# Two-layer diffusion block on one core: the modulation's weight product made by scaled copies and additions instead of matmuls

## The chip, the core and the metric

The kernel runs on one core of a Trainium2 chip. The core has a matrix engine (TensorE, PE in the profile, with its weight loads as PEld), VectorE (DVE), ScalarE (ACT), GpSimd (POOL) and SyncE (SP, which here only issues DMAs). Each engine works through its own queue in order and waits on semaphores for the others. TensorE reads from SBUF and writes to PSUM; GpSimd reads and writes SBUF only. The metric is the time of one execution on the device in microseconds, lower is better.

## What is computed

Two layers of a block: a modulated RMSNorm, one wide input projection that feeds a state-space scan and a differential attention, two gated branch projections, an output projection, and a modulated gated FFN with a short convolution. There are 256 latent tokens and 256 context tokens; both go through the same weights in layer 0, and in layer 1 the context is only read. All data is fp32. The change concerns the modulation, which is a product of a vector with a large matrix:

```python
for i in range(DEPTH):
    mod_l = (jax.nn.silu(c) @ w_mod[i] + b_mod[i])[:, None, :]
    mod_c = (jax.nn.silu(c_ctx) @ w_mod[i] + b_mod[i])[None, None, :]
    sh1_l, sc1_l, g1_l, sh2_l, sc2_l, g2_l = jnp.split(mod_l, N_MOD, axis=-1)
    ...
```

`w_mod[i]` has 1024 rows and 6144 columns (25 MB a layer). `c` and `c_ctx` are the two conditions. The second, small part of the change is in the scan: for each chunk of 128 tokens it needs the running sum of `a` in both directions and the sums over the rest of the chunk (`a_cs` and `a_cs[..., -1:] - a_cs` in the reference's `ssd_scan`).

## The kernel before

**Projections.** A projection takes its weights in tiles of 4 blocks of 128 rows by 256 columns (512 KB). `load_w` issues a tile's DMA on SP's queue (buffers `raw`, 3), `split_w` makes a rounded copy `whi` on ACT (L313) and the rest `wlo` on DVE (L314), 3 buffers each, and the gemm helpers (L384 to L445) run three matmuls per block of rows: high by high, high by low, low by high. `plan` lists all tiles in order. `take` hands tiles to a gemm, keeps `DL` = 2 tiles loaded or ready ahead, and calls `drip` once for each tile. A tile of 512 tokens is 24 matmuls of 512 columns.

**What runs between.** `lanes` are two queues of generators (attention heads, scan groups) that a gemm advances by `pump` after every second block of rows; so heads and scan run in between the projections' matmuls. `trickle` is a third queue, advanced by `drip`: it holds the modulation.

**The modulation.** The first third of a layer's columns (`g` = 0) of layer 0 is made at the start (`boot_mod`). The other five groups of 2048 columns, two of layer 0 and the first of layer 1 during layer 0 and two during layer 1, are made by `mod_part` (L457). `s2` holds for each block of 128 rows the two conditions after their activation as two columns among 32, the others zero. One step loads a block of 128 rows by 1024 columns (`mraw`, 512 KB, 2 buffers) and does 4 fp32 matmuls (L465), each with 32 columns of `s2` as weights and 256 columns of the block moving, into 4 bands of 32 partitions of the PSUM bank `pmmod`; 16 steps sum one group. An fp32 matmul is two records in the trace, so a step is 8. Then the bank is copied to `modrow`, transposed in four pieces (L472) and added to the bias. Five groups are 80 steps.

**Order.** The instructions of each engine are ordered by a scheduling framework that follows the program's order where it can; attention and scan matmuls (`pmm`, `ptr`, L85 and L88) are kept in program order. No queue is reordered at run time.

**Stages.** Layer 0: start (0 to 66 us of the span), attention with the Q, K and V projections (to 235), the "dt block", a short chain that makes the step sizes and the triangle sums `p1` (L817 to L863, near 235 to 250), the B, C and gate projections and the attention's branch projection (to 425), the scan with the XS, gate and Z projections (to 590), the last gates and the scan's branch projection (to 665), then output projection and FFN. Layer 1 begins near 1097 and goes the same way, with 256 tokens in most projections. `flush` empties `trickle` at the end of the scan's branch projection.

Of the kernel before, what the change touches and what calls it, by code (L numbers as in the profile page):

```python
# [10 lines left out]
F32 = mybir.dt.float32  # L11
# [21 lines left out]
C_ID, C_ONE, C_LE, C_GE, C_GT, C_LT, C_COS, C_SIN = 0, 128, 256, 384, 512, 640, 768, 1024  # L33
C_W = 1280


def shape_constants():
    a = np.zeros((P, C_W), np.float32)
    i = np.arange(P)
    r, s = i[:, None], i[None, :]  # L40
    a[:, C_ID:C_ID + P] = r == s
    a[:, C_LE:C_LE + P] = r <= s
    a[:, C_GE:C_GE + P] = r >= s
    a[:, C_GT:C_GT + P] = r > s
    a[:, C_LT:C_LT + P] = r < s
# [14 lines left out]
def hybrid_backbone_kernel(  # L60
# [36 lines left out]
    strict = (kt[:, C_GT:C_GT + P], kt[:, C_LT:C_LT + P])  # L97
# [3 lines left out]
    V.memset(mhalf, -0.5)  # L101

# [226 lines left out]
    trickle = []  # L329

# [29 lines left out]
    def take(n_tiles):  # L360
# [5 lines left out]
        for _ in range(n_tiles):  # L366
            drip()
# [89 lines left out]
    def mod_part(i, g, pool, ps):  # L457

        for half in range(2):
            for k in range(KD):  # L460
                raw = pool.tile([P, 4, 256], F32, tag="mraw", name=nm("mraw"), bufs=2)
                src = w_mod[i, k * P:(k + 1) * P, g * 2048:(g + 1) * 2048]
                nc.sync.dma_start(raw, src.rearrange("p (j h n) -> p h j n", j=4, h=2)[:, half])
                for j in range(4):
                    T.matmul(ps[32 * j:32 * j + 32, half * 256:half * 256 + 256], s2[:, k, :], raw[:, j, :],  # L465
                             start=k == 0, stop=k == KD - 1)
                yield 1
        row = lp.tile([P, 512], F32, tag="g", name=nm("modrow"), bufs=4)
        A.copy(row, ps)
        pt = bank("s")  # L470
        for b in range(4):
            T.transpose(pt[:, b * P:(b + 1) * P], row[:, b * P:(b + 1) * P], ident)  # L472
        m = col[i]["mod"]
        for v in range(2):
            V.tensor_tensor(
                m[:, g * 16:(g + 1) * 16, v].rearrange("p (j b) -> p b j", j=4),
                pt.rearrange("p (b j r) -> p b j r", b=4, j=4)[:, :, :, v],
                col[i]["bm"][:, g * 16:(g + 1) * 16].rearrange("p (j b) -> p b j", j=4), op=ALU.add)
        if g == 0:
            a, sc, nw = col[i]["a1"], m[:, 8:16, :], col[i]["n1"]  # L480
        elif g == 2:
            a, sc, nw = col[i]["a2"], m[:, 32:40, :], col[i]["n2"]
        else:
            return
        V.scalar_tensor_tensor(a, sc, 1.0, nw.unsqueeze(2).to_broadcast([P, KD, 2]), op0=ALU.add, op1=ALU.mult)
# [89 lines left out]
    for i in range(DEPTH):  # L575
# [75 lines left out]
        trickle.extend(mod_part(*lg, mp, mb) for lg in (((0, 1), (0, 2), (1, 0)) if full else ((1, 1), (1, 2))))  # L651
# [17 lines left out]
        spare[:] = ["mm"]  # L669
        ast = ExitStack()  # L670
# [141 lines left out]


# [5 lines left out]
        if True:  # L819
# [24 lines left out]
            for n, lhs in enumerate((tri[0], tri[1], strict[0], strict[1])):  # L844
                T.matmul(p1[:, n * P:(n + 1) * P], lhs, av, start=True, stop=True)
            T.matmul(p2[:, 0:P], ones, av, start=True, stop=True)
            p1v = p1.rearrange("p (n t c) -> p n t c", n=4, t=4)
# [42 lines left out]

        spare[:] = ["mm"]
# [154 lines left out]
        spare[:] = ["mm", "s"]  # L1046
        rst = ExitStack()
# [159 lines left out]
```

## Time and profile before

| | us |
|---|---|
| median of 3 runs | 1742.55 |
| lowest, highest | 1740.89, 1753.69 |
| profiled execution, its own time | 1740.01 |
| its span, first to last instruction | 1738.2 |
| TensorE clock granted in it, mean | 0.993 |

The busy time of an engine is the union of its instructions' times, without waits. A group's row has the line, the engine, the operation, output and inputs, the shapes and a count; then busy time and mean of one in ns; then the idle time of the engine just before these instructions, and who ended it. In a row of windows each engine has its busy time in that stretch and a count of instructions. A tile's row has the shortest, median and longest duration in ns. The end of a matmul is modelled, so what it holds PE for is read from one start to the next.

### The profile page before, as it was taken

The numbers are of one execution on the slowest core, as the hardware profiler recorded it, in microseconds if no ns is written. First come the engines' busy times: TensorE is split into PE (matmuls) and PEld (weight loads), VectorE is DVE, ScalarE is ACT, GpSimd is POOL, SyncE is SP. The second block draws the span as 40 slices with busy tenths as digits, with TensorE's granted clock in tenths as the row PEclk, the third lists the DMA queues.
The fourth block names the chain that finished last, engine by engine and source line by source line (L and its number), as shares of the span: only waits on it lengthen the run. The fifth ranks groups of instructions, "written<-read, shape, count | busy, mean of one in ns | idle before, by whom it ended". The sixth has DMA issues, their size and how long they took to land. (4 is left out here: it accounts for less than half of the span.)

```text
span 1738.2 us, 27022 instructions
## 1 busy us (share of the span) xinstructions
PE 1667.1 (96%) x10547; PEld 1406.2 (81%) x10547; DVE 1148.0 (66%) x2008; ACT 848.2 (49%) x1567; POOL 181.3 (10%) x212
## 2 busy tenths in 40 slices
PE   7999999999988999999999999999999898989997
PEld 4788878777766788888888888788879788989997
DVE  4776667325988855766666326666675789779964
ACT  3565665413545423644444225555655455466653
POOL 3000010001433000300000002100000252010000
PEclk9999999999999999999999999999999999989999
DMA  9644333555443234233323335844535445646653
GB/s 317 215 127 126 115 119 108 166 173 146 121 107 100 74 109 146 74 97 97 97 87 95 92 108 161 255 146 146 152 93 171 121 110 144 199 154 185 193 176 117
DMA packets 233199, 240.71 MB, mean 138 GB/s; under 512 B 10908, under 2 KB 223551, under 8 KB 233071
## 3 DMA queue, kind: packets, MB, share of 16 engines
q1 hardware_dynamic: 230720, 237.14, 45.4%
q8 instruction: 83, 1.36, 0.3%
q0 software_dynamic: 1312, 1.03, 0.2%
q10 hardware_dynamic: 1039, 0.81, 0.1%
q14 instruction: 45, 0.37, 0.1%
HBM read 234.62 MB, written 4.33 MB: 137 GB/s over the span
## 5 line engine op out<-in xcount | busy, mean ns | idle before, releaser
L314 DVE TENSOR_TENSOR wlo<-raw,whi 128x1024 fp32r<-128x1024 f32 (+1 forms) x318 | 388.3, 1221 | 255.7 <-ACT whi L313 254.8
L313 ACT CAST whi<-raw 128x1024 fp32r<-128x1024 f32 (+1 forms) x318 | 329.2, 1036 | 378.4 <-PE pmmmm L408 146.6
L407 PE MATMUL pmmmm<-th,whi 128*128 128x512 f32 x744 | 306.3, 412 | 1.6 <-DVE chv L572 1.6
L408 PE MATMUL pmmmm<-tl,whi 128*128 128x512 f32 x744 | 296.5, 399 | 0.0
L409 PE MATMUL pmmmm<-th,wlo 128*128 128x512 f32 x744 | 295.6, 397 | 0.0
L407 PEld LDWEIGHTS pmmmm<-th,whi 128*128 128x128 f32 x744 | 140.5, 189 | 42.2 <-issue 7.9
L409 PEld LDWEIGHTS pmmmm<-th,wlo 128*128 128x128 f32 x744 | 140.4, 189 | 34.5 <-issue 1.0
L408 PEld LDWEIGHTS pmmmm<-tl,whi 128*128 128x128 f32 x744 | 140.5, 189 | 31.0 <-issue 2.2
L393 PE MATMUL pmmmm<-th,whi 128*128 128x256 f32 x480 | 138.5, 289 | 1.5 <-ACT whi L313 1.3
L395 PE MATMUL pmmmm<-th,wlo 128*128 128x256 f32 x480 | 134.7, 281 | 0.6 <-DVE wlo L314 0.6
L394 PE MATMUL pmmmm<-tl,whi 128*128 128x256 f32 x480 | 134.8, 281 | 0.0
L969 POOL TENSOR_TENSOR cs<-cs,csc 128x512 f32<-128x512 f32 x48 | 69.1, 1454 | 264.0 <-DMA cs<-csd 141.5
L393 PEld LDWEIGHTS pmmmm<-th,whi 128*128 128x128 f32 x480 | 90.7, 189 | 6.2 <-issue 3.8
L394 PEld LDWEIGHTS pmmmm<-tl,whi 128*128 128x128 f32 x480 | 90.8, 189 | 0.7 <-issue 0.4
L395 PEld LDWEIGHTS pmmmm<-th,wlo 128*128 128x128 f32 x480 | 90.6, 189 | 0.8 <-DVE wlo L314 0.8
L409 PE MATMUL psmm<-th,wlo 128*128 128x512 f32 x200 | 79.3, 397 | 0.0
L725 ACT ACTIVATE e<-psscore,nmx 128x512 f32<-128x512 f32 (+1 forms) x96 | 58.1, 610 | 43.5 <-DVE nmx L722 40.5
L408 PE MATMUL psmm<-tl,whi 128*128 128x512 f32 x200 | 79.2, 396 | 0.0
L521 POOL TENSOR_TENSOR rs<-ms,mhalf 128x2 f32<-128x2 f32 x9 | 6.3, 699 | 698.5 <-DVE ms L518 698.5
L407 PE MATMUL psmm<-th,whi 128*128 128x512 f32 x200 | 79.0, 395 | 0.0
L722 DVE TENSOR_REDUCE nmx<-psscore 128x1 f32<-128x512 f32 (+1 forms) x80 | 51.8, 684 | 34.3 <-PE psscore L85 34.2
L441 PE MATMUL pmmmm<-whi,th 128*128 128x256 f32 x256 | 74.3, 290 | 0.0
(346 smaller groups left out, 3899.0 us busy)
## 6 DMA issues: line engine op xcount, KB each, us to landing
raw<-in_w_in_dram SPq DMA_DIRECT2D x124, 512.0 KB, 4.0
raw<-in_w_up_dram SPq DMA_DIRECT2D x88, 512.0 KB, 3.6
mraw<-in_w_mod_dram SPq DMA_DIRECT2D x80, 512.0 KB, 4.7
raw<-in_w_down_dram SPq DMA_DIRECT2D x45, 512.0 KB, 3.6
cs<-csd SPq DMA_DIRECT2D x24, 512.0 KB, 5.8
boot<-in_w_mod_dram SPq DMA_DIRECT2D x16, 512.0 KB, 9.3
raw<-in_w_br_att_dram SPq DMA_DIRECT2D x16, 512.0 KB, 3.6
raw<-in_w_br_ssd_dram SPq DMA_DIRECT2D x16, 512.0 KB, 3.5
```

What stands on the lines that cost most here:

```text
L313: pin(A.copy(hi[:, 0:n, :], raw[:, 0:n, :]))
L314: pin(V.tensor_tensor(lo[:, 0:n, :], raw[:, 0:n, :], hi[:, 0:n, :].bitcast(F32), op=ALU.subtract))
L393: T.matmul(o[f], whi[:, kk, cs], xh, start=first, stop=False)
L394: T.matmul(o[f], whi[:, kk, cs], xl, start=False, stop=False)
L395: T.matmul(o[f], wlo[:, kk, cs], xh, start=False, stop=last)
L407: T.matmul(o, whi[:, k % 4, cs], hi[k][:, 0:n], start=k == 0, stop=False)
L408: T.matmul(o, whi[:, k % 4, cs], lo[k][:, 0:n], start=False, stop=False)
L409: T.matmul(o, wlo[:, k % 4, cs], hi[k][:, 0:n], start=False, stop=k == k_tiles - 1)
L441: T.matmul(b[:, n, :], hi[k][:, ts], whi[:, k % 4, :], start=k == 0 and n == 0, stop=False)
L722: V.tensor_reduce(nmx[:, cc, 0:ng], sc[cc].rearrange("p (g k) -> p g k", g=ng), axis=AX.X, op=ALU.max, negate=True)
L725: A.activation(e[cc][:, g * w:(g + 1) * w], sc[cc][:, g * w:(g + 1) * w], AF.Exp, bias=nmx[:, cc, g:g + 1], accum_out=sm[:, cc, g:g + 1])
L969: G.tensor_tensor(cs[:, dr], cs[:, dr], csc[:, t, 16 * dr + 4 * g:16 * dr + 4 * g + 4].unsqueeze(2).to_broadcast([P, 4, P]), op=ALU.subtract)
```

## The change

`mod_part` no longer multiplies on TensorE. It takes the 2048 columns of a group in 4 blocks of 512. For each of the 8 blocks of 128 rows it loads 128 rows by 512 columns (`mraw`, 256 KB, 2 buffers), and ACT multiplies this tile by a condition: each partition's row by that partition's value of `s2`, a copy with a column as scale. The first row block's products go straight into the sum `macc`; from then on GpSimd adds each product to `macc`. With two conditions (`nv` = 2) the first product goes to a scratch tile `mt` (1 buffer) and the second back into `mraw`; with one it goes into `mraw`. So a step is one DMA, `nv` products and `nv` additions (none at the first row block). After 8 steps 4 matmuls with `pick` as weights (one column of ones among zeros, shifted so that the four blocks fall on different partitions) sum `macc` over its partitions. `macc` has one buffer. A group is 32 steps instead of 16, each with half the bytes. In layer 1 only the latent condition is made (`nv` = 1).

`pace` sets how many steps are advanced: `drip` is called `pace`/2 times per weight tile. It is 4 in the attention of layer 0, 3 until the scan, 0 in the scan, 4 from the end of the scan until layer 1 sets 3.

In the dt block two of four triangle products go: the strict sums are the other triangle's sums less the value itself, two subtractions on DVE and one exponential where there were two.

```diff
@@ shape_constants and its use: the two strict triangles go, the constant is 1024 wide instead of 1280
+    pick = base.tile([P, 64], F32, name="pick")
+    V.memset(pick, 0.0)
+    V.memset(pick[:, 32:33], 1.0)
...
         for _ in range(n_tiles):
-            drip()
+            owed[0] += pace[0]
+            while owed[0] >= 2:
+                owed[0] -= 2
+                drip()
...
-    def mod_part(i, g, pool, ps):
+    def mod_part(i, g, pool, ps, nv):
-        for half in range(2):
+        for q in range(4):
+            acc = pool.tile([P, nv, 512], F32, tag="macc", name=nm("macc"), bufs=1)
             for k in range(KD):
-                raw = pool.tile([P, 4, 256], F32, tag="mraw", name=nm("mraw"), bufs=2)
-                src = w_mod[i, k * P:(k + 1) * P, g * 2048:(g + 1) * 2048]
-                nc.sync.dma_start(raw, src.rearrange("p (j h n) -> p h j n", j=4, h=2)[:, half])
-                for j in range(4):
-                    T.matmul(ps[32 * j:32 * j + 32, half * 256:half * 256 + 256], s2[:, k, :], raw[:, j, :],
-                             start=k == 0, stop=k == KD - 1)
-                yield 1
+                raw = pool.tile([P, 512], F32, tag="mraw", name=nm("mraw"), bufs=2)
+                c0 = g * 2048 + q * 512
+                nc.sync.dma_start(raw, w_mod[i, k * P:(k + 1) * P, c0:c0 + 512])
+                yield 1
+                for v in range(nv):
+                    sum_ = acc[:, v, :]
+                    if k == 0:
+                        dst = sum_
+                    elif v == nv - 1:
+                        dst = raw
+                    else:
+                        dst = pool.tile([P, 512], F32, tag="mt", name=nm("mt"), bufs=1)
+                    A.activation(dst, raw, AF.Copy, scale=s2[:, k, v:v + 1])
+                    if k:
+                        G.tensor_tensor(sum_, sum_, dst, op=ALU.add)
+            w = 128 * nv
+            for j in range(4):
+                T.matmul(ps[32 * j:32 * j + 32, 0:w], pick[:, 32 - q:64 - q],
+                         acc.rearrange("p v n -> p (v n)")[:, j * w:(j + 1) * w], start=q == 0, stop=q == 3)
...
-        for b in range(4):
+        for b in range(nv):
             T.transpose(pt[:, b * P:(b + 1) * P], row[:, b * P:(b + 1) * P], ident)
...
+        pace[0] = 4 if full else 3
...
-            for n, lhs in enumerate((tri[0], tri[1], strict[0], strict[1])):
+            for n, lhs in enumerate(tri):
                 T.matmul(p1[:, n * P:(n + 1) * P], lhs, av, start=True, stop=True)
...
-                A.activation(ddt[:, :, cs], p1v[:, 2 + dr, :, cs], AF.Exp)
+                V.tensor_tensor(ddt[:, :, cs], p1v[:, 1 - dr, :, cs], av[:, :, cs], op=ALU.subtract)
+            A.activation(ddt, ddt, AF.Exp)
```

The rest of the program stands on TensorE almost as it did. Three places show what moved; the line numbers are those of the changed file in the second fence of each pair (there L481 is the product, L483 the addition, L487 the `pick` matmul, L471 and L305 the DMAs of `mraw` and `raw`, L314 the cast `whi`, L748 the softmax's exponential, L702 and L704 the copies of Q and K, L765 the copy of the transposed probabilities).

ACT in the attention of layer 0, from the copies of one pair of Q or K blocks on: before,

```order
L679 ACTIVATE rraw_953<-pmmmm_884 128x256
L681 ACTIVATE qk_952<-pmmmm_884 128x256
L313 CAST whi_1023<-raw_866 128x1024
L725 ACTIVATE e_977,sm_976<-psscore_969,nmx_975 128x512
L725 ACTIVATE e_978,sm_976<-psscore_970,nmx_975 128x512
L742 COPY pT_1004<-psattT_999 128x512
L313 CAST whi_1041<-raw_1021 128x1024
```

and after:

```order
L702 ACTIVATE rraw_1164<-pmmmm_1091 128x256
L704 ACTIVATE qk_1163<-pmmmm_1091 128x256
L481 ACTIVATE mt_1237<-mraw_1085,s_128 128x512
L481 ACTIVATE mraw_1085<-mraw_1085,s_128 128x512
L748 ACTIVATE e_1157,sm_1156<-psscore_1149,nmx_1155 128x512
L481 ACTIVATE mt_1244<-mraw_1242,s_128 128x512
L748 ACTIVATE e_1158,sm_1156<-psscore_1150,nmx_1155 128x512
L314 CAST whi_1231<-raw_1055 128x1024
L765 COPY pT_1194<-psattT_1189 128x512
L481 ACTIVATE mraw_1242<-mraw_1242,s_128 128x512
L481 ACTIVATE mt_1251<-mraw_1249,s_128 128x512
L481 ACTIVATE mraw_1249<-mraw_1249,s_128 128x512
```

Products now stand between the exponentials of a head and ahead of the weight casts; each `mt` waits for the addition of the one before. Counted over the whole order, 82 products stand ahead of the dt block, 80 between it and the scan, 30 behind the scan and 64 in layer 1.

SP in the same stage: before,

```order
L304 DMA raw_1021<-in_w_in_dram 128x4x256
L463 DMA mraw_1029<-in_w_mod_dram 128x4x256
L304 DMA raw_1027<-in_w_in_dram 128x4x256
L463 DMA mraw_1035<-in_w_mod_dram 128x4x256
L304 DMA raw_1183<-in_w_in_dram 128x4x256
```

and after:

```order
L305 DMA raw_1235<-in_w_in_dram 128x4x256
L471 DMA mraw_1085<-in_w_mod_dram 128x512
L471 DMA mraw_1242<-in_w_mod_dram 128x512
L471 DMA mraw_1249<-in_w_mod_dram 128x512
L471 DMA mraw_1256<-in_w_mod_dram 128x512
L305 DMA raw_1454<-in_w_in_dram 128x4x256
L471 DMA mraw_1263<-in_w_mod_dram 128x512
```

One modulation DMA per weight DMA became up to four in a row, and each of them waits until GpSimd has done the last addition from its buffer.

TensorE in the same stage: before,

```order
L408 MATMUL pmmmm_961<-tl_261,whi_862 128x512
L409 MATMUL pmmmm_961<-th_260,wlo_863 128x512
L465 MATMUL pmmod_604<-mraw_1029,s_125 32x256 x4
L465 MATMUL pmmod_604<-mraw_1035,s_125 32x256 x4
L407 MATMUL pmmmm_1045<-th_246,whi_880 128x512
```

and after:

```order
L448 MATMUL pmmmm_1375<-whi_1231,tl_264 128x256
L449 MATMUL pmmmm_1375<-wlo_1232,th_263 128x256
L487 MATMUL pmmod_607<-macc_1066,pick 32x256 x4
L413 MATMUL pmmmm_1496<-th_249,whi_1265 128x512
L414 MATMUL pmmmm_1496<-tl_250,whi_1265 128x512
```

The pairs of four matmuls of every two tiles are gone; four `pick` matmuls stand once per eight steps, and wait for GpSimd's last addition into that `macc`.

More of the change, by code (lines that the diff above doesn't have):

```diff
@@ L30 @@
     0, 1024, 2048, 2560, 3072, 3104, 4128, 5152, 6176, 7200)
-C_ID, C_ONE, C_LE, C_GE, C_GT, C_LT, C_COS, C_SIN = 0, 128, 256, 384, 512, 640, 768, 1024
-C_W = 1280
+C_ID, C_ONE, C_LE, C_GE, C_COS, C_SIN = 0, 128, 256, 384, 512, 768
+C_W = 1024
 def shape_constants():
@@ L96, in hybrid_backbone_kernel @@
     tri2 = kt[:, C_LE:C_LE + 2 * P].rearrange("p (d l) -> p d l", d=2)
-    strict = (kt[:, C_GT:C_GT + P], kt[:, C_LT:C_LT + P])
     cosT = kt[:, C_COS:C_COS + SEQ]
@@ L329, in hybrid_backbone_kernel @@
     trickle = []
+    pace = [3]
+    owed = [0]
     def advance(queue):
@@ L468, in mod_part @@
         row = lp.tile([P, 512], F32, tag="g", name=nm("modrow"), bufs=4)
-        A.copy(row, ps)
+        A.copy(row[:, 0:w], ps[:, 0:w])
         pt = bank("s")
-        for b in range(4):
+        for b in range(nv):
             T.transpose(pt[:, b * P:(b + 1) * P], row[:, b * P:(b + 1) * P], ident)
         m = col[i]["mod"]
-        for v in range(2):
+        for v in range(nv):
             V.tensor_tensor(
-                m[:, g * 16:(g + 1) * 16, v].rearrange("p (j b) -> p b j", j=4),
-                pt.rearrange("p (b j r) -> p b j r", b=4, j=4)[:, :, :, v],
-                col[i]["bm"][:, g * 16:(g + 1) * 16].rearrange("p (j b) -> p b j", j=4), op=ALU.add)
+                m[:, g * 16:(g + 1) * 16, v].rearrange("p (q h b) -> p b h q", q=4, b=nv),
+                pt[:, 0:nv * P].rearrange("p (b v h r) -> p b v h r", b=nv, v=nv, r=32)[:, :, v, :, 0:4],
+                col[i]["bm"][:, g * 16:(g + 1) * 16].rearrange("p (q h b) -> p b h q", q=4, b=nv), op=ALU.add)
@@ L479, in mod_part @@
         if g == 0:
-            a, sc, nw = col[i]["a1"], m[:, 8:16, :], col[i]["n1"]
+            a, sc, nw = col[i]["a1"], m[:, 8:16, 0:nv], col[i]["n1"]
         elif g == 2:
-            a, sc, nw = col[i]["a2"], m[:, 32:40, :], col[i]["n2"]
+            a, sc, nw = col[i]["a2"], m[:, 32:40, 0:nv], col[i]["n2"]
         else:
             return
-        V.scalar_tensor_tensor(a, sc, 1.0, nw.unsqueeze(2).to_broadcast([P, KD, 2]), op0=ALU.add, op1=ALU.mult)
+        V.scalar_tensor_tensor(a[:, :, 0:nv], sc, 1.0, nw.unsqueeze(2).to_broadcast([P, KD, nv]), op0=ALU.add, op1=ALU.mult)
@@ L650, in hybrid_backbone_kernel @@
         mb = bank("m", "mod")
-        trickle.extend(mod_part(*lg, mp, mb) for lg in (((0, 1), (0, 2), (1, 0)) if full else ((1, 1), (1, 2))))
+        trickle.extend(mod_part(*lg, mp, mb, 2 if full else 1)
+                       for lg in (((0, 1), (0, 2), (1, 0)) if full else ((1, 1), (1, 2))))
         mg = [mp.tile([P, N], F32, name=f"mg{i}_{j}") for j in range(KD)]
@@ L810, in hybrid_backbone_kernel @@
                 lanes[f].append(attend(2 * p + f, qk[f], qk[2 + f], vT, f * P))
+        pace[0] = 3
         ps = bank("mm", "dt")
@@ L888, in hybrid_backbone_kernel @@
         ast.close()
+        pace[0] = 0
         spare[:] = ["mm"]
@@ L1046, in hybrid_backbone_kernel @@
         spare[:] = ["mm", "s"]
+        pace[0] = 4
         rst = ExitStack()
```

4 lines of the change are left out of this document (1 added, 3 removed).

## The prediction, made before the changed kernel was run

> **What bounds the kernel now.** I read the page first, for the busy times and the chain that ended last; then the windows, which give the busy time of each engine by stage; then the same windows for the modulation's matmuls alone; and last the timeline and single groups for prices.
>
> ```profile
> span 1738.2 us, 27022 instructions
> PE 1667.1 (96%) x10547; PEld 1406.2 (81%) x10547; DVE 1148.0 (66%) x2008; ACT 848.2 (49%) x1567; POOL 181.3 (10%) x212
> PE 30%; issue 3%; DVE 2%; DMA 2%; POOL 1%; ACT 1%; POOLq 0%; DVEq 0%; ACTq 0%; SPq 0%
> ...
> core 0: us, PE busy (x) PEld busy (x) DVE busy (x) ACT busy (x) POOL busy (x), PEclk, DMA share, GB/s
> 66.00:235.00 169.00, 168.19 (x1167) 141.67 (x1169) 122.78 (x266) 107.97 (x258) 4.62 (x5) 1.00 0.43 133
> 235.00:425.00 190.00, 188.27 (x1035) 144.29 (x1027) 90.22 (x140) 76.63 (x147) 13.46 (x16) 1.00 0.49 150
> 425.00:590.00 165.00, 148.14 (x880) 116.31 (x880) 139.07 (x245) 81.97 (x165) 54.81 (x52) 0.98 0.40 105
> 590.00:665.00 75.00, 74.43 (x323) 59.85 (x323) 44.32 (x75) 26.72 (x43) 1.40 (x2) 1.00 0.32 103
> 1097.00:1302.00 205.00, 202.35 (x1453) 166.23 (x1446) 135.97 (x283) 116.63 (x242) 9.04 (x15) 1.00 0.52 156
> ```
>
> TensorE (PE) is the bound: 96% busy over the span, and in four of these five stages it is idle for 0.6 to 2.7 us. The stages are the attention of layer 0 (66 to 235), its B/C/gate/attention projections (235 to 425), its scan (425 to 590), its last gates and scan projection (590 to 665), and the front half of layer 1 (1097 to 1302). The reader should keep the third one: there VectorE (DVE) is busy 139.07 of 165 us (84%) and GpSimd (POOL) 54.81, and PE has fallen to 148.14, which is 90%. That is what a crowded stage costs in this kernel. The first, where much of the new work goes, has ScalarE (ACT) at 64% and DVE at 73% already.
>
> **What the change takes from PE.** The same windows for the modulation's matmuls alone, one pair of steps in the timeline, and the group:
>
> ```profile
> core 0: us, PE busy (x) PEld busy (x) ACT busy (x), PEclk, DMA share, GB/s
> 66.00:235.00 169.00, 10.91 (x160) 4.08 (x160) 0.57 (x1) 1.00 0.43 133
> 235.00:425.00 190.00, 15.58 (x224) 6.06 (x224) 0.58 (x1) 1.00 0.49 150
> 1097.00:1302.00 205.00, 19.52 (x256) 5.63 (x248) 0.58 (x1) 1.00 0.52 156
> ...
> 91.23 1.05 ACT L313 CAST whi<-raw 128x1024 fp32r<-128x1024 f32 x1
> 91.32 1.07 PE L465 MATMUL pmmod<-mraw,s 128*32 128x256 f32 x16
> 92.19 0.38 ACT L679 ACTIVATE rraw<-pmmmm 128x256 f32<-128x256 f32 x1
> 92.32 0.50 PE L407 MATMUL pmmmm<-th,whi 128*128 128x512 f32 x1
> ...
> L465 PE MATMUL pmmod<-mraw,s 128*32 128x256 f32 x640 | 46.3, 387 | 2.6 <-DMA mraw<-in_w_mod_dram 2.5
> ```
>
> The 80 steps before (five groups of 16, each step 4 fp32 matmuls, which are 8 records) cost 10.9 + 15.6 + 19.5 = 46.0 us of PE. The pair at 91.32 holds PE for exactly 1.00 us until L407 starts, so the least is 80 x 0.50 = 40; the most is 46.3 + 2.6 idle for the weight's DMA = 48.9. I take 46.0, since most of layer 1's steps stand alone and cost 19.52 / 32 = 0.61.
>
> After it, PE gets 4 matmuls for each of 4 column blocks of a group: 12 blocks with both conditions (same shape as L465, so 0.61 each: 7.3 us) and 8 blocks of layer 1 with one (128 columns; between half and all of 0.61, I take 0.4: 3.2 us). Net: 46.0 - 10.5 = 35.5 us off PE (range 29 to 41).
>
> ```profile
> L845 PE MATMUL ps<-dtT,kt x16: 273/275/377, 246.1 to 1271.7; 128*128 128x128 f32 x16
> L472 PE MATMUL ps<-kt,modrow x20: 269/272/328, 196.1 to 1303.3; 128*128 128x128 f32 x20
> ```
>
> Small edits together: 8 of the 16 triangle records (L845) and 12 of the 20 transposes of the modulation's rows go. They are pipelined; at 0.1 to 0.27 us each that is 2 to 5 us, and I take 2. The strict sums now come from the other triangle less the value itself: two short DVE subtractions for one ACT exponential, beside the B/C projections and not needed before the scan, so nothing. The smaller constant and the memsets lie in the start's loads: nothing. If all new work hid, the profiled execution (1740.0 us; its span 1738.2 plus 1.8 around it; the median of the runs shown is 2.5 us above it) would come to 1740.0 - 35.5 - 2 = 1702.5.
>
> **What it adds elsewhere.** Prices for one product on ACT (128x512, scale from a column) and for one addition on POOL:
>
> ```profile
> L725 ACT ACTIVATE e<-psscore,nmx 128x512 f32<-128x512 f32 x24 | 16.3, 685 | 18.4 <-DVE nmx L722 15.5 <-DVE qk L686 2.9
> L742 ACT COPY pT<-psattT 128x512 f32<-128x512 f32 x18 | 10.5, 583 | 16.7 <-PE psattT L88 16.7
> L701 ACT CAST KS<-qk 64x512 fp32r<-64x512 f32 x16 | 9.9, 619 | 0.4
> ...
> L969 POOL TENSOR_TENSOR cs<-cs,csc x48: 1031/1319/2108, 417.8 to 1457.3; 128x512 f32<-128x512 f32 x48
> ```
>
> A column operand costs 685 - 583 = 0.10, a copy from SBUF 0.62, so a product takes 0.72; queued instructions overlap by 0.09 (the cast at 91.23 would end at 92.28, the next starts at 92.19), so 0.63 in a full queue. An addition takes 1.03 alone, 1.3 at the median, 2.1 at worst.
>
> Attention of layer 0: in the order of the changed kernel 82 products stand ahead of the dt block. 82 x 0.63 = 52 us on top of 108.0, so ACT needs 160 us (150 where its present work packs as tightly), and PE needs 169 - 10.9 + 4 x 0.61 = 161. ACT thus stands at 93 to 99% of the stage. POOL gets about 70 additions, 72 us alone and 91 at the median. DVE has 122.8 us of its own and meets POOL:
>
> ```profile
> 508.26 4.06 POOL L969 TENSOR_TENSOR cs<-cs,csc 128x512 f32<-128x512 f32 x2 [2.30 <-ACT cc L966]
> 509.69 1.73 DVE L314 TENSOR_TENSOR wlo<-raw,whi 128x1024 fp32r<-128x1024 f32 x1
> 511.35 1.25 DVE L935 TENSOR_TENSOR h<-h,etot 128x256 f32<-128x256 f32 x1
> ...
> L935 DVE TENSOR_TENSOR h<-h,etot 128x256 f32<-128x256 f32 x32 | 14.1, 443 | 0.3 <-ACT h L933 0.3
> ...
> L314 DVE TENSOR_TENSOR wlo<-raw,whi 128x1024 fp32r<-128x1024 f32 x21 | 25.6, 1221 | 6.9 <-ACT whi L313 6.7 <-PE ps L472 0.2
> ```
>
> Two additions took 4.06 us instead of 2.06, while L314 took 1.73 instead of 1.22 and L935 1.25 instead of 0.44: both sides wait. So the stage has three nearly full engines. Between ends far apart (161, all hidden; 195, the rival below) the nearest row is the scan's, 90% of PE at 84% of DVE; here ACT is fuller still, so I take 89%: 161 / 0.89 = 181, 20 us given back.
>
> The other stages have room. 235 to 425: 80 products, ACT 76.6 + 50 = 127 of 190 - 15.6 + 5 x 0.61 = 177. 590 to 665: 30 products, ACT 26.7 + 19 = 46 of 76. Layer 1: 64 products (one condition), ACT 116.6 + 40 = 157 of 205 - 19.5 + 3.2 = 189, 56 additions of about 1.3 beside DVE's 136. At each of the 20 column blocks PE's four matmuls wait for POOL's last addition, with every later projection matmul queued behind them in PE's order. Nothing like that is in the trace; bounds are 0 and one whole addition (2.1 x 20 = 42), and I take 0.3 each, since the order puts work between: 6 us. It also covers the small power operations of the attention heads (rsa), which now queue behind additions on POOL. The modulation's DMAs are twice as many, half as long, on SP's queue ahead of weight loads; they hold those only until POOL frees a buffer, and a weight is loaded two tiles ahead: nothing, with the fourth case below as the price if that cover is gone.
>
> Sum: 1740.0 - 37.5 + 20 + 6 = 1728.5; I say 1728.
>
> **Where the skill speaks against it.** The page "SBUF — State Buffer" of the Trainium skill (section Who interferes with whom) says that a VectorE instruction with two SBUF inputs and a GpSimd instruction that reads SBUF exclude each other for their whole length. The rows at 508 us agree (1.25 for 0.44). By that rule every addition that starts first stops such an instruction outright, and the sum would be the third case's, 1743, where my 89% gives 1728.
>
> **The rivals.** *All hidden*: the order spaces the products between other ACT work, and ACT's idle time ahead of L725 and L742 (18.4 and 16.7 us) is waiting for DVE and PE, which products can fill. Against it stands 93 to 99% for an engine that works in order. 1703.
>
> *No change, VectorE and GpSimd exclude each other*: if each of the 70 additions keeps DVE for its 1.03 us, DVE needs 122.8 + 72 = 195 in the attention stage, PE waits there, 34 us are given back, and 1702.5 + 34 + 6 = 1743. For it: the rows at 508. Against: part of DVE's work there has at most one SBUF input and need not meet POOL, first of all the two forms of the score's maximum:
>
> ```profile
> L722 DVE TENSOR_REDUCE nmx<-psscore 128x1 f32<-128x512 f32 x24 | 15.7, 684 | 10.3 <-PE psscore L85 10.2
> L722 DVE TENSOR_REDUCE nmx<-psscore 128x2 f32<-128x512 f32 x12 | 7.7, 681 | 5.7 <-PE psscore L85 5.7
> ```
>
> *Slower, the chain of a step holds SP's queue*: two raw buffers, each filled by a DMA, multiplied on ACT, added on POOL before it is free.
>
> ```profile
> raw<-in_w_down_dram SPq DMA_DIRECT2D x9, 256.0 KB, 3.1
> DMA to landing us min/median/max: 3.6/4.7/6.7
> ```
>
> A DMA of 256 KB lands in 3.1 us; with 1.4 for two products and 1.4 for the last addition, two steps take 5.9, 3.0 each. The attention stage has 41 steps in 161 us, 3.9 each, so that holds. With the 4.7 us that a modulation load took (512 KB), 1.4 of products and both additions at 2.1, two steps take 10.3, 5.15 each. Then weight loads wait on SP: 41 x 1.25 = 51 there, 40 x (5.15 - 4.4) = 30 in the next stage, and 1702.5 + 81 = 1784. It decides against the change from 4.6 us a step (41 x 0.7 + 40 x 0.2 = 37).
>
> **How the numbers follow.** The forecast, most of it given back in the attention of layer 0 (1715 to 1740): 0.45. All hidden (1702 to 1715): 0.25. Exclusion (1740 to 1758): 0.17. The held queue: 0.13. The range 1704 to 1757 leaves out the last and the edges of the others. One per cent, about what a measurement of this kernel can tell from no change, is 1725 to 1760. Faster: 0.25 and 0.4 of the forecast's 0.45, 0.43. Slower: 0.13. The rest, 0.44, within.
>
> **What would show it.** PE's busy time for pmmod near 10 us. The window of layer 0's attention (up to the dt block): 181 us if I am right, 161 if all hides, 195 under exclusion. ACT above 85% busy there, L314's mean above 1.3 us, an addition's mean near 1.3. PE idle before the pick matmuls about 6 us in all, ended by POOL. Wrong if weight splits wait for DMA (held queue), or if PE in that stage stays above 97%.

## The result, and the profile after

The changed kernel is slower: 1831.04 us, median of 4 runs (1825.02 to 1834.21), beside 1742.19 for the kernel before in the same session. The ratio is 1.0491, with a 95% interval of 1.0438 to 1.0543. The forecast of 1728 and its whole range lie below this.

The busy times on the page of the changed kernel (its profiled execution took 1830.07 us):

```profile
span 1828.3 us, 26847 instructions
PE 1674.7 (92%) x10047; PEld 1420.8 (78%) x10047; DVE 1254.2 (69%) x2012; ACT 1008.0 (55%) x1821; POOL 502.6 (27%) x436
```

Four things stand in the second line. PE executes 500 records fewer than before and yet is busy 7.6 us longer. VectorE (DVE) executes 2012 instructions where it had 2008, and is busy 106.2 us longer. GpSimd (POOL) is busy 321 us longer, for 224 additions that my prediction priced at 1.3 us, 291 in all. ScalarE (ACT) is as busy as forecast: 160 us more for 256 products.

The groups of DVE and POOL that answer this, of the kernel before and then of the changed one (line, engine, operation, tiles, shapes, count; busy us, mean ns of one; idle time ahead):

```profile
L314 DVE TENSOR_TENSOR wlo<-raw,whi 128x1024 fp32r<-128x1024 f32 x309 | 381.6, 1235 | 237.4 <-ACT whi L313 236.5 <-PE ps L472 0.2
L733 DVE SCALAR_TENSOR_TENSOR e<-e,sm,e 128x512 f32<-128x512 f32 x32 | 23.9, 745 | 0.6
L732 DVE TENSOR_SCALAR e<-e,sm 128x512 f32<-128x512 f32 x32 | 15.3, 477 | 0.0
L686 DVE TENSOR_TENSOR qk<-rraw,rsw 128x256 f32<-128x256 f32 x32 | 13.4, 419 | 0.4
L572 DVE SCALAR_TENSOR_TENSOR chv<-pmmmm,cols,chv 128x510 f32<-128x510 f32 x28 | 20.8, 742 | 0.3
```

```profile
L315 DVE TENSOR_TENSOR wlo<-raw,whi 128x1024 fp32r<-128x1024 f32 x309 | 410.3, 1328 | 237.2 <-ACT whi L314 235.7 <-PE psattT L86 1.0
L756 DVE SCALAR_TENSOR_TENSOR e<-e,sm,e 128x512 f32<-128x512 f32 x32 | 30.5, 952 | 0.4
L755 DVE TENSOR_SCALAR e<-e,sm 128x512 f32<-128x512 f32 x32 | 20.7, 647 | 0.0
L709 DVE TENSOR_TENSOR qk<-rraw,rsw 128x256 f32<-128x256 f32 x32 | 25.0, 782 | 0.4
L593 DVE SCALAR_TENSOR_TENSOR chv<-pmmmm,cols,chv 128x510 f32<-128x510 f32 x28 | 20.7, 741 | 0.4
L745 DVE TENSOR_REDUCE nmx<-psscore 128x1 f32<-128x512 f32 x64 | 42.2, 682 | 15.6 <-PE psscore L83 15.6
L483 POOL TENSOR_TENSOR macc<-macc,mraw 128x512 f32<-128x512 f32 x140 | 204.6, 1461 | 145.9 <-ACT mraw L481 91.9 <-ACT macc L481 40.1 <-PE ps L493 8.1
L483 POOL TENSOR_TENSOR macc<-macc,mt 128x512 f32<-128x512 f32 x84 | 119.1, 1417 | 175.8 <-ACT mt L481 127.2 <-ACT macc L481 48.3
```

Compare row with row. The instructions that read two tiles from SBUF became longer: the rotation's addition (`qk`) from 419 to 782 ns, the mixing of the two softmaxes (`e<-e,sm,e`) from 745 to 952, the weight split (`wlo`) from 1235 to 1328 over all its 309. So did `e<-e,sm`, with one SBUF tile, from 477 to 647. Two kinds did not move: `chv`, which reads one of its tiles from PSUM (742, 741), and the maximum over PSUM (684 and 681 in the rows of the prediction, 682 now). A slower engine would have moved all of them. Nor did these two merely miss the additions: in the timeline at least 14 of the 64 maxima and 5 of the 28 `chv` run while an addition is under way, at 0.68 and 0.74 us in the mean. Of the weight splits that stand alone in it, 48 meet an addition and take 1.73 us, and 255 meet none and take 1.24.

The timelines of POOL and of DVE in the changed kernel show one such meeting (start us, length us):

```profile
187.25 1.65 POOL L483 TENSOR_TENSOR macc<-macc,mt 128x512 f32<-128x512 f32 x1 [10.13 <-ACT macc L481]
188.85 1.49 POOL L483 TENSOR_TENSOR macc<-macc,mraw 128x512 f32<-128x512 f32 x1
...
188.15 1.03 DVE L707 TENSOR_TENSOR rsw<-rsw,kt 128x256 f32<-128x256 f32 x1
189.10 1.51 DVE L708 TENSOR_TENSOR rraw<-rraw,kt 128x256 f32<-128x256 f32 x1
190.65 0.42 DVE L709 TENSOR_TENSOR qk<-rraw,rsw 128x256 f32<-128x256 f32 x1
```

L707, L708 and L709 are three instructions of the same size. L707 starts while the first addition runs and ends 0.28 us after it (189.18 against 188.90); L708 starts in the second and ends 0.27 us after it (190.61 against 190.34); L709 meets none and takes 0.42. The 1.03 us of L707 are counted as busy, so this cost hides in the busy column: nothing in it looks like waiting.

Where the time went, by stages of the changed kernel (the windows of the attention of layer 0, its B/C/gate/attention projections, its scan projection and the front of layer 1; the first runs from the first score matmul to the first copy of `dtr`, the start of the dt block):

```profile
core 0: us, PE busy (x) PEld busy (x) DVE busy (x) ACT busy (x) POOL busy (x), PEclk, DMA share, GB/s
85.30:273.30 188.00, 162.99 (x954) 134.72 (x952) 147.69 (x242) 148.22 (x323) 98.09 (x67) 0.92 0.35 106
273.30:475.90 202.60, 179.70 (x809) 141.18 (x810) 115.58 (x139) 126.15 (x220) 110.90 (x86) 0.93 0.40 121
663.70:730.10 66.40, 57.08 (x227) 42.65 (x226) 36.04 (x38) 30.71 (x43) 35.37 (x24) 0.90 0.40 125
1214.50:1452.10 237.60, 214.22 (x1448) 189.31 (x1446) 168.80 (x288) 156.50 (x307) 73.02 (x62) 0.97 0.49 140
```

No engine is full in the first stage: PE 87%, DVE 79%, ACT 79%, POOL 52%. The granted clock, 1.00 in four of the five windows before, is 0.90 to 0.97. Over the whole program the mean granted clock went from 0.993 to 0.964. The three longest entries of PE's waits are these (time in all, times, longest):

```profile
PE pmmod L487 <- POOL macc L483: 30.6, 13, 6.2
PE psattT L86 <- DVE e L756: 22.9, 15, 3.8
PE psattT L86 <- DVE on L781: 8.6, 2, 4.5
```

My first reading was that the pick matmuls (`pmmod`) were at the root, with the clock as amplifier. The experiments did not bear that out.

### The profile page after: what moved, and what is told of

The parts are those of the page before. It is cut to its first block, busy times and chain, and to the rows that moved or that the text cites. A ratio compares the mean times of both kernels' runs of the same rounds, so it can differ in the third digit from the quotient of the medians.

```text
span 1828.3 us, 26847 instructions
## 1 busy us (share of the span) xinstructions
PE 1674.7 (92%) x10047; PEld 1420.8 (78%) x10047; DVE 1254.2 (69%) x2012; ACT 1008.0 (55%) x1821; POOL 502.6 (27%) x436
## 3 DMA queue, kind: packets, MB, share of 16 engines
q0 software_dynamic: 1312, 1.03, 0.2%
## 5 line engine op out<-in xcount | busy, mean ns | idle before, releaser
L315 DVE TENSOR_TENSOR wlo<-raw,whi 128x1024 fp32r<-128x1024 f32 (+1 forms) x318 | 417.0, 1312 | 255.6 <-ACT whi L314 254.1
L314 ACT CAST whi<-raw 128x1024 fp32r<-128x1024 f32 (+1 forms) x318 | 328.1, 1034 | 282.4 <-PE pmmmm L400 107.9
L413 PE MATMUL pmmmm<-th,whi 128*128 128x512 f32 x744 | 311.5, 419 | 4.3 <-DVE chv L593 4.3
L415 PE MATMUL pmmmm<-th,wlo 128*128 128x512 f32 x744 | 300.9, 404 | 5.3 <-DVE wlo L315 5.3
L414 PE MATMUL pmmmm<-tl,whi 128*128 128x512 f32 x744 | 301.2, 405 | 0.0
L483 POOL TENSOR_TENSOR macc<-macc,mraw 128x512 f32<-128x512 f32 x140 | 204.6, 1461 | 145.9 <-ACT mraw L481 91.9
L413 PEld LDWEIGHTS pmmmm<-th,whi 128*128 128x128 f32 x744 | 144.0, 194 | 41.8 <-issue 9.4
L414 PEld LDWEIGHTS pmmmm<-tl,whi 128*128 128x128 f32 x744 | 144.5, 194 | 31.1 <-issue 0.9
L483 POOL TENSOR_TENSOR macc<-macc,mt 128x512 f32<-128x512 f32 x84 | 119.1, 1417 | 175.8 <-ACT mt L481 127.2
L481 ACT ACTIVATE mraw<-mraw,s 128x512 f32<-128x512 f32 x140 | 101.1, 723 | 33.4 <-DMA mraw<-in_w_mod_dram 31.7
L481 ACT ACTIVATE mt<-mraw,s 128x512 f32<-128x512 f32 x84 | 60.7, 723 | 67.1 <-DMA mraw<-in_w_mod_dram 60.2
L399 PEld LDWEIGHTS pmmmm<-th,whi 128*128 128x128 f32 x480 | 91.0, 190 | 4.8 <-ACT whi L314 2.9
L400 PEld LDWEIGHTS pmmmm<-tl,whi 128*128 128x128 f32 x480 | 91.1, 190 | 0.5 <-issue 0.3
```

What stands on the lines that cost most here:

```text
L314: pin(A.copy(hi[:, 0:n, :], raw[:, 0:n, :]))
L315: pin(V.tensor_tensor(lo[:, 0:n, :], raw[:, 0:n, :], hi[:, 0:n, :].bitcast(F32), op=ALU.subtract))
L399: T.matmul(o[f], whi[:, kk, cs], xh, start=first, stop=False)
L400: T.matmul(o[f], whi[:, kk, cs], xl, start=False, stop=False)
L413: T.matmul(o, whi[:, k % 4, cs], hi[k][:, 0:n], start=k == 0, stop=False)
L414: T.matmul(o, whi[:, k % 4, cs], lo[k][:, 0:n], start=False, stop=False)
```

## The experiments

All ratios are to the kernel before, measured beside it on the same chip. The names are those of the runs.

**Pick later.** The four `pick` matmuls of a block are issued two steps later:

```diff
-            for j in range(4):
-                T.matmul(ps[...], pick[...], acc[...], start=q == 0, stop=q == 3)
+            late.append(lambda q=q, acc=acc: pick_sums(q, acc))
...
+                if k == 1:
+                    settle()
```

> The changed kernel with the four `pick` matmuls of a column block issued two steps of the modulation later (the first product of the next block waits for them). Nothing is left out. Theory W (PE stands still at the pick matmuls because it works in order): the 30.6 us that PE idles there for POOL's last addition fall below 8 us, and the 30.9 us at half clock that follow directly on such waits go too, which is worth about 15 us: 1830 - 23 - 15 = about 1790 (1780 to 1800). Rival C (the attention's chains of DVE and ACT are late anyway, the pick wait only shows where PE would idle in any case): the idle time moves to `psattT` and `psscore` rows, and the time is 1815 to 1835.

Measured: 1835.41 us, ratio 1.0502 (1.0484 to 1.0521), which is no change against the changed kernel. But its own purpose failed, as the same entry of PE's waits shows:

```profile
PE pmmod L475 <- POOL macc L504: 24.3, 13, 4.6
```

24.3 of 30.6 us remained, since the sums were later still. So it refuted neither theory, and I took the wait away for good in the next one.

**Pick without waiting.** The pick matmuls read a constant in place of the sums:

```diff
-                         acc.rearrange("p v n -> p (v n)")[:, j * w:(j + 1) * w], start=q == 0, stop=q == 3)
+                         kt[:, 0:w], start=q == 0, stop=q == 3)
```

> The changed kernel with the pick matmuls reading a constant tile in place of the sums, so that TensorE never waits for POOL's last addition (the modulation is then wrong); products, additions and DMAs are all as in the changed kernel. In the run with late picks 24.3 of the 30.6 us of waits were still there, so that it did not tell. If TensorE's wait at the picks is a cause of its own, the 30.6 us and about 15 us of half clock after them go: 1780 to 1800. If VectorE's stretched instructions set the pace and the pick waits only show where TensorE would stand anyway, at most a third of it: 1812 to 1835.

Measured: 1828.00 us, ratio 1.0456 (1.0432 to 1.0481). That is 0.0035 below the changed kernel, 6 us, with overlapping intervals. PE's longest waits are now others, and the idle time has moved:

```profile
PE psattT L86 <- DVE e L756: 25.9, 15, 4.2
PE psscore L83 <- ACT e L748: 8.3, 4, 3.3
PE pmmmm L415 <- DVE wlo L315: 8.2, 5, 3.7
```

So the pick waits show where PE stands when DVE and POOL are late; they are not why it does.

**Products alone, additions alone, neither.** Three kernels leave out POOL's additions, ScalarE's products, or both, after the first row block:

```diff
-                    if k:
-                        G.tensor_tensor(sum_, sum_, dst, op=ALU.add)
```
```diff
-                    elif v == nv - 1:
+                    else:
                         dst = raw
-                    else:
-                        dst = pool.tile([P, 512], F32, tag="mt", name=nm("mt"), bufs=1)
-                    A.activation(dst, raw, AF.Copy, scale=s2[:, k, v:v + 1])
+                    if k == 0:
+                        A.activation(dst, raw, AF.Copy, scale=s2[:, k, v:v + 1])
```
```diff
-                for v in range(nv):
+                for v in range(nv if k == 0 else 0):
```

> The changed kernel with all of POOL's additions of the modulation left out (the products on ScalarE stay; the modulation is then wrong from the second row block on). Theory P (POOL's additions delay DVE and PE): the attention of layer 0 (188 us long in the changed kernel, 154.5 before) falls to below 165, the pick waits to below 3 us in all, and the time to 1705 to 1730. Theory A (ScalarE's products crowd the attention's copies and exponentials): the attention stays at 175 us or more, and only the pick waits with their half clock go: 1775 to 1800.

> The changed kernel with ScalarE's products left out after the first row block; POOL adds the raw weight tile as often as before (the modulation is then wrong). Theory A (ScalarE's products crowd the attention): the attention of layer 0 falls to below 165 us, and the time to 1730 to 1770, since POOL's additions start earlier too and the pick waits shrink. Theory P (POOL's additions are what delays): the attention stays at 175 us or more, and the time at 1795 to 1830.

> The changed kernel with products and additions both left out after the first row block; all DMAs of the modulation, the pick matmuls and the smaller triangle work stay. This is the floor that my prediction called all hidden, 1702.5 (1698 to 1709). If the twice as many DMAs on SP's queue cost something by themselves, it stays above 1715, with PE waiting at weight splits for DMA. If PE's half clock is only a consequence of waits, half-clock time is back to about 30 us.

| kernel | time, us | ratio (95% interval) |
|---|---|---|
| neither | 1705.56 | 0.976 (0.9733 to 0.9787) |
| products alone | 1737.93 | 0.9946 (0.9923 to 0.997) |
| additions alone | 1802.62 | 1.0317 (1.0288 to 1.0346) |
| both (the changed kernel) | 1831.04 | 1.0491 (1.0438 to 1.0543) |

The attention of layer 0 takes 162.4 us with products alone and 175.7 with additions alone, against 149.0 with neither: a part of each theory's delay is there, 13 us for the products and 27 for the additions. Accordingly the time with products alone lies above theory P's 1705 to 1730 and far below theory A's 1775 to 1800. The floor is where the prediction had it, so the DMAs, twice as many, cost nothing that shows. From there, with 1742 us to the ratio, the products cost 0.0186, 32 us, the additions 0.0557, 97 us; together that makes 129, and both at once cost 127. Within the intervals the two burdens simply add up, and three quarters is POOL's. The windows of the kernel with neither, in the same four stages:

```profile
80.00:229.00 149.00, 147.28 (x954) 125.61 (x952) 111.83 (x240) 102.43 (x251) 4.06 (x4) 1.00 0.47 140
229.00:405.20 176.20, 169.09 (x810) 135.06 (x810) 88.17 (x139) 80.98 (x151) 14.00 (x16) 1.00 0.47 141
595.50:645.60 50.10, 50.10 (x226) 39.24 (x225) 27.33 (x36) 16.28 (x21) 0.00 (x0) 1.00 0.40 126
1116.80:1329.30 212.50, 208.10 (x1448) 185.00 (x1447) 147.95 (x289) 129.29 (x264) 16.59 (x20) 1.00 0.55 159
```

Against these the changed kernel is longer by 39.0, 26.4, 16.3 and 25.1 us, 106.8 of the 123.5 between the two spans, and DVE's busy time in them is longer by 35.9, 27.4, 8.7 and 20.9 with the same work.

**Why additions cost more than their time.** Either they exclude DVE, or they are late links in a chain (buffers freed late, sums late). I replaced each by two memsets on the same two tiles, so that POOL still takes the same place and frees the same buffers, but reads nothing:

```diff
-                        G.tensor_tensor(sum_, sum_, dst, op=ALU.add)
+                        G.memset(dst, 0.0)
+                        G.memset(sum_, 0.0)
```

> The changed kernel with each of POOL's additions replaced by two memsets of POOL on the same two tiles (a memset of 64x512 took 0.52 us, so about as long together as an addition alone, 1.03): POOL is as busy, frees the buffers as late and is waited for at the same places, but it reads nothing from SBUF. The modulation is then wrong. Theory E (exclusion: an addition stops VectorE instructions that read two SBUF tiles, and is stopped by them): VectorE's qk additions fall back from 782 to about 420 ns, the weight splits to about 1235, and the time to that without additions, 1735 to 1755. Theory Q (it is POOL's place in the chain, buffers and sums that come late, with POOL's time): the attention of layer 0 stays above 180 us and the time above 1800.

Measured: 1742.90 us, ratio 0.9975 (0.995 to 1.0), that is 0.0516 or 90 us below the changed kernel, and 5 us above products alone. Its groups:

```profile
L315 DVE TENSOR_TENSOR wlo<-raw,whi 128x1024 fp32r<-128x1024 f32 x309 | 382.0, 1236 | 233.0 <-ACT whi L314 230.8 <-PE psattT L86 1.6
L757 DVE SCALAR_TENSOR_TENSOR e<-e,sm,e 128x512 f32<-128x512 f32 x32 | 23.8, 745 | 0.4
L756 DVE TENSOR_SCALAR e<-e,sm 128x512 f32<-128x512 f32 x32 | 19.6, 613 | 0.0
L710 DVE TENSOR_TENSOR qk<-rraw,rsw 128x256 f32<-128x256 f32 x32 | 13.4, 418 | 0.4
L484 POOL MEMSET macc<- 128x512 f32 x224 | 112.7, 527 | 84.5 <-ACT macc L481 81.2
```

Two memsets take 1.06 us, an addition alone 1.03. The rows with two SBUF inputs are back at their length of before (1236, 745, 418), and 90 of the additions' 97 us are gone. It is not that they no longer meet POOL: 17 of the 32 `qk` run while a memset is under way, at 0.42 us in the mean. The exclusion is shown, for both sides at once: the additions' own stretching, from 1.03 to about 1.44 us, goes with it, and this kernel does not part the two. One row stayed long: `e<-e,sm`, 613 ns. Sixteen of its 32 meet a memset, and two of these, at 1.82 and 2.87 us, make up most of the difference. The page "SBUF — State Buffer" of the Trainium skill (Who interferes with whom) separates the two cases in this way: an instruction with two SBUF inputs meets only a GpSimd instruction that reads SBUF, while a `tensor_scalar` in its two-port mode takes the shared pair of ports against any. The trace agrees, with 418 and 613.

The same four stages in the kernel with memsets:

```profile
79.50:246.00 166.50, 152.54 (x956) 127.74 (x954) 115.91 (x244) 146.50 (x324) 65.53 (x126) 0.98 0.41 122
246.00:424.40 178.40, 170.24 (x807) 135.86 (x807) 91.37 (x138) 125.26 (x222) 86.16 (x159) 0.99 0.45 138
616.60:666.90 50.30, 50.30 (x227) 39.33 (x226) 27.32 (x36) 24.01 (x33) 12.76 (x26) 1.00 0.38 121
1139.80:1364.90 225.10, 212.23 (x1449) 185.97 (x1448) 148.06 (x289) 156.12 (x309) 61.61 (x106) 0.99 0.54 155
```

They are 17.5, 2.2, 0.2 and 12.6 us longer than with neither. So in the second and third stage products and POOL's place in the chain cost next to nothing, and nearly all of the 26.4 and 16.3 us is the exclusion; in the first and last about half of the 39.0 and 25.1 is.

**The same sums without POOL.** Product and addition in one DVE instruction, from the second row block on:

```diff
                     if k == 0:
-                        dst = sum_
-                    elif v == nv - 1:
-                        dst = raw
+                        A.activation(sum_, raw, AF.Copy, scale=s2[:, k, v:v + 1])
                     else:
-                        dst = pool.tile([P, 512], F32, tag="mt", name=nm("mt"), bufs=1)
-                    A.activation(dst, raw, AF.Copy, scale=s2[:, k, v:v + 1])
-                    if k:
-                        G.tensor_tensor(sum_, sum_, dst, op=ALU.add)
+                        V.scalar_tensor_tensor(sum_, raw, s2[:, k, v:v + 1], sum_, op0=ALU.mult, op1=ALU.add)
```

> The changed kernel with product and addition done by one VectorE instruction (scalar_tensor_tensor) from the second row block on, in place of ScalarE and POOL. Nothing is left out. 224 instructions of about 0.745 us (the row of e<-e,sm,e) add 167 us to VectorE, but nothing excludes it. Theory E: no VectorE row is stretched, the stage of layer 0's attention is bounded by VectorE at 120 + 72 x 0.745 = 174 us (149 without the modulation), and the time comes to 1735 to 1775, below the changed kernel by more than 50. Theory Q: the sums still come late; 1800 or more.

Measured: 1730.85 us, ratio 0.9892 (0.9852 to 0.9932): a few us better than expected, and 1.1% faster than the kernel before. The attention of layer 0 takes 157.8 us with DVE busy 145.9 of them; the expectation's 174 us, with DVE as the bound, did not come about. The new group:

```profile
L478 DVE SCALAR_TENSOR_TENSOR macc<-mraw,s,macc 128x512 f32<-128x512 f32 x224 | 160.5, 744 | 34.7 <-DMA mraw<-in_w_mod_dram 31.8 <-ACT macc L476 2.1
```

224 instructions take 160.5 us of DVE, against 106.2 us by which POOL's additions had lengthened it (and 323.7 us of POOL, 161.8 of ACT). In the two profiles DVE's total is even 29 us higher than in the changed kernel, 1283.5 against 1254.2; the time is 100 us lower. So DVE's total does not tell the time. Two burdens go at once here, POOL's additions and most of ScalarE's products, which cost 97 and 32 us above; what takes their place costs 0.0132 of the time over the floor, 23 us. That this is because nothing is stopped midway is argued; no run parts it from the ease for ScalarE.

**Triangles alone.** The kernel before with the triangle edit only:

```diff
-            for n, lhs in enumerate((tri[0], tri[1], strict[0], strict[1])):
+            for n, lhs in enumerate(tri):
...
-                A.activation(ddt[:, :, cs], p1v[:, 2 + dr, :, cs], AF.Exp)
+                V.tensor_tensor(ddt[:, :, cs], p1v[:, 1 - dr, :, cs], av[:, :, cs], op=ALU.subtract)
+            A.activation(ddt, ddt, AF.Exp)
```

> The kernel before with only the triangle edit of the change (two products fewer, the strict sums by subtraction on VectorE). Nothing is left out. My prediction gave this edit, with the transposes that are not touched here, 2 us: so 0 to 3 us faster, ratio 0.998 to 1.000. If the strict sums were waited for, 2 us or more slower.

Measured: 1747.70 us, ratio 0.9997 (0.9983 to 1.001). That cannot be told from no change.

**Moving layer 1's part into the FFN.** From the kernel before, layer 1's groups are summed in layer 0's FFN, where PE is the only full engine: all three by one DVE instruction each, or two of them by ScalarE and POOL as in the change. The diff is that of the first, shortened.

```diff
-        trickle.extend(mod_part(*lg, mp, mb) for lg in (((0, 1), (0, 2), (1, 0)) if full else ((1, 1), (1, 2))))
+        if full:
+            trickle.extend(mod_part(*lg, mp, mb) for lg in ((0, 1), (0, 2)))
...
+        if full:
+            mf = fst.enter_context(tc.tile_pool(name=f"mf{i}", bufs=1))
+            mb = bank("m", "mod")
+            trickle.extend(mod_sum(*lg, mf, mb) for lg in ((1, 0, 0), (1, 0, 1), (1, 1, 0), (1, 2, 0)))
+            trickle.append(mod_end())
```

> A version meant to beat both: the kernel before with two triangles fewer and layer 1's three groups taken off TensorE and out of the attention stages; one VectorE instruction per product and addition, during layer 0's FFN, where TensorE is busy 100%, VectorE 56% and POOL nearly 0; layer 0's two groups stay on TensorE. Nothing is left out. TensorE loses 48 steps of 0.5 to 0.6 us (24 to 29) and gets 16 blocks of 4 small matmuls (4 to 8): 1742 - 20 - 2 = 1720 (1712 to 1728) if VectorE, then at about 88% there, hides it; above 1742 if VectorE then delays TensorE in the FFN.

> As h1, but only the two groups (1,1) and (1,2) with one condition, with ScalarE's products and POOL's additions as in the change, in layer 0's FFN; the three groups of layer 0's list stay on TensorE. Nothing is left out. TensorE loses 32 steps (16 to 19) and gets 8 blocks (2 to 4): 1742 - 14 - 2 = 1726 (1720 to 1732) if the cover of the FFN is enough. By theory E the weight splits in the FFN are stretched (56 additions, up to 1 us each), but VectorE stands at 56% there, so that it costs nothing; if it does cost, 1735 to 1750.

Both missed, by my own counting: 1839.22 us, ratio 1.0513 (1.0482 to 1.0544), and 1816.75 us, ratio 1.0373 (1.0337 to 1.0409). PE's longest wait in the first:

```profile
PE pmmod L495 <- DVE macc L532: 105.8, 8, 13.7
```

One step is issued for each weight tile, and the FFN has half as many tiles as I took; in the trace 64 of the first kernel's 128 sums run behind the FFN's last matmul, in `flush`, where PE stands still for 8 blocks of some 13 us. In the second the same waits, for POOL, are 74.3 us in 4 blocks. That says nothing on the idea, so I mended the pace, and started from the version with one DVE instruction for product and addition (`e7_fused`; the diff, shortened, is from it to `h5`): `h4` moves (1,1) and (1,2), `h5` all three, (1,0) in a pass for each condition, so that its weights are loaded twice. `drip` is called `pace`/4 times per weight tile in both.

```diff
-        trickle.extend(mod_part(*lg, mp, mb, 2 if full else 1)
-                       for lg in (((0, 1), (0, 2), (1, 0)) if full else ((1, 1), (1, 2))))
+        if full:
+            trickle.extend(mod_part(*lg, mp, mb, 2) for lg in ((0, 1), (0, 2)))
...
+            trickle.extend(mod_sum(*lg, mf, mb) for lg in ((1, 0, 0), (1, 0, 1), (1, 1, 0), (1, 2, 0)))
+            pace[0], owed[0] = 9, 0
```

> The version with product and addition in one VectorE instruction (e7_fused), and layer 1's two groups (1,1) and (1,2) moved into layer 0's FFN, where VectorE is busy 56%: 64 instructions of 0.75 us, one or two a weight tile, so that all are done before the last tiles (in h1 69 steps were left over at the end of the FFN and TensorE stood still for them). Nothing is left out. In e7 the front of layer 1 took 13 us longer than in e4_loads; these go: 1731 - 12 = 1719 (1712 to 1726). If VectorE in the FFN then delays the weight splits, 1731 or more.

> As h4, with group (1,0) moved into layer 0's FFN too (128 instructions there, in two passes, one for each condition), and layer 0's two groups spread more thinly over its attention. Nothing is left out. VectorE comes to 56% + 96 / 290 = 89% in the FFN; the attention of layer 0, 8.7 us longer in e7 than in e4_loads, comes down by about 6: 1713 (1705 to 1722). If VectorE at 89% delays TensorE, 1725 or more.

Measured: 1723.18 us, ratio 0.9847 (0.9823 to 0.987), and 1721.68 us, ratio 0.9843 (0.9819 to 0.9867). Both beat both kernels by their whole intervals; between the two there is no difference that can be told. The first came as expected; the second ends at the upper edge of its range, and the 6 us that it was to gain beyond the first are not there. The second's FFN in two windows:

```profile
800.00:900.00 100.00, 99.66 (x459) 78.24 (x458) 85.42 (x118) 42.39 (x54) 0.00 (x0) 1.00 0.61 190
900.00:1000.00 100.00, 100.00 (x459) 78.56 (x459) 75.24 (x104) 33.16 (x45) 0.00 (x0) 1.00 0.64 197
```

DVE works 85% and 75% there and PE hardly waits: 99.66 and 100.00. The sums are not free all the same: from its first convolution instruction on DVE to its last matmul this FFN takes 380.2 us, and 368.4 in the kernel before, and PE is busy for 10.6 of these 11.8 us, 6.4 of them in the matmuls that end the sums. What is left to the floor is 0.008 of the time, 14 us.

## Why the prediction was wrong, step by step

**What leaves PE** was right. "All hidden", 1702.5, was built as a kernel and measured 1705.56 beside 1747.09 for the kernel before (1700 by its ratio). PE's busy time for `pmmod` there is 11.05 us, forecast 10.5. Of the 2 us for triangles and transposes nothing can be seen for the triangles; the transposes were not tried alone.

**The durations** were right for ACT: 0.72 us a product, 0.72 measured. An addition was forecast at 1.3 and took 1.46 and 1.42.

**The attention of layer 0** was the first wrong term. I took 181 us, by a PE share of 89% from the scan's row, and gave back 20; against the floor 39 were given back. (My 181 counts from 66 us. By the marks of the windows above the stage takes 154.5 us in the kernel before, 14.5 less than my 169, so 166.5 is what stands beside the measured 188.0.) A share of PE taken from another stage has no term for the mechanism. The third rival, exclusion, came to 34 with its 195. It named the mechanism, from the rows at 508 us, and I gave it 0.17 because part of DVE's work reads one SBUF tile at most. That is true of the maxima, which kept their length, and it was too little to matter. That its 34 lie near the 39 is in part luck: 13 us of delay here come with the products alone, and 27 with the additions alone.

**"The other stages have room" was the step that failed most.** It compares sums of busy time, ACT 127 of 177 and so on, and gives nothing back there. Against the floor, 26.4, 16.3 and 25.1 us were given back in those stages, 67.8 together. Room in the sum did not help, since an addition does not go where DVE is idle: it goes when its product is ready, and it holds up the instructions with two SBUF inputs that meet it. With memsets, where the products and POOL's instructions are all in place but the exclusion is gone, 2.2 and 0.2 us are given back in the first two of them: there the step lacked the exclusion and nothing else. In layer 1 12.6 us stay, so there it was wrong without the exclusion too. Nor did I carry the exclusion to the stages after the first when I priced the rival, so 1743 was far too low as well, and so was the upper end of the range, 1757.

**The waits at the pick matmuls** were forecast at 6 us of PE idle, and 30.6 are shown. Taken away, they are worth 6 (0.0035), with overlapping intervals. So their price cannot be told from nothing, and that it comes out at my 6 is luck; the idle column would have put it five times too high.

**ScalarE** I had at 93 to 99% of the attention, and above 85% as a sign; in the changed kernel it is at 79% of a longer stage. In the kernel with products alone it is:

```profile
79.90:242.30 162.40, 151.27 (x956) 128.03 (x954) 113.12 (x238) 147.28 (x324) 4.53 (x5) 0.98 0.41 124
```

147.28 of 162.40 us, 91%, in a stage 13 us longer than the floor's. So the effect was there, some 32 us over the program. That it comes from ACT's queue being full is argued from this share; no run parts it from other effects of the products.

**The held queue** was not it. The kernel with memsets keeps the whole chain of a step (DMA, products, POOL), its modulation DMAs wait for POOL for 333.6 us where they waited 354.5, and it is 90 us faster all the same. In the changed kernel ACT's casts of weights wait for PE; for a weight's DMA they wait once, 4.2 us. The longest of ACT's waits:

```profile
ACT whi L314 <- PE pmmmm L400: 107.9, 54, 5.0
ACT whi L314 <- PE pmmmm L414: 72.4, 59, 3.4
ACT whi L314 <- PE psmm L400: 63.3, 45, 7.3
ACT mt L481 <- DMA mraw<-in_w_mod_dram: 60.2, 39, 4.7
```

The last row is the products' wait for their own weights. It is 54.5 us with products alone too, so it belongs to the products' 32 us, not to the additions.

**What the prediction left out** is PE's clock. The windows of the changed kernel around two waits at a pick:

```profile
427.00:430.80 3.80, 1.26 (x7) 0.33 (x5) 0.77 (x1) 3.18 (x4) 3.80 (x4) 1.00 0.24 70
430.80:434.20 3.40, 3.26 (x9) 2.01 (x10) 2.90 (x3) 2.13 (x4) 0.09 (x1) 0.50 0.39 108
434.20:438.00 3.80, 3.80 (x18) 3.02 (x17) 0.00 (x0) 1.25 (x3) 2.54 (x2) 1.00 0.93 303
```

After 2.07 and 0.61 us without work, the clock is 0.50 for 3.4 us: in that time the same matmuls start 0.43 us apart, behind it 0.23. With a mean of 0.964 over 1828.3 us, and the two levels 1.00 and 0.50, that is 132 us at half clock (24 before, by 0.993). It explains why PE is busy longer with less work. The kernel with neither has the same 10047 records and is busy 1630.1 us, 44.6 less; by its 0.988 it has 41 us at half clock, 91 less, and half of that, 45, is the most that these can cost. So the slow clock accounts for up to a third of the 123.5 us between the two spans. It is a consequence: where the waits went, in the kernel with memsets, the mean is 0.984 and PE is busy 1647.5 us.

## What to carry to other kernels

Before work is given to an idle GpSimd, look at what VectorE runs beside it: here an addition over SBUF held up the VectorE instructions with two SBUF inputs that met it (0.42 us became 1.03 and 1.51), and the profile shows that as busy time, in longer means of unchanged instructions. Sums of busy time did not tell whether a stage had room for such work. That it has room where VectorE can be late is argued; the run that was to show it, with ScalarE and POOL in the FFN, was lost to the count of tiles. One fused VectorE instruction did the same work for a gain of 1.1%, and of 1.5% with layer 1's part in a stage where the matrix engine alone is full.

## What the runs showed of the hardware

That a memset of POOL, 0.53 us for 128x512, leaves DVE's instructions with two SBUF inputs at their length (418 and 745 ns) and still stretches `tensor_scalar` with one (477 to 613), I had not expected. Nor had I expected PE's clock to halve after so short a wait. The page "TensorE: Matmul & The Clock Gate" of the Trainium skill (Part 1) gives an idle window of about 3.4 us for that; here 2.07 and 0.61 us with little work between were enough. That this slow stretch lasts 3.4 us and has the clock at exactly one half agrees with the page. In the trace all 25 slow stretches of the changed kernel but the last, which the end of the program cuts, last 3.4 us or a whole multiple of it, up to 13.7; in the 3.4 us before each, PE is idle for 1.7 to 3.4 us.
